# Seven products instead of eight in more pairs of a feed-forward layer, with sums made by accumulating transfers

## The chip, the cores and the metric

The kernel runs on one core of a Trainium2 chip. A core has TensorE (PE in the profile; its weight loads are PEld), VectorE (DVE), ScalarE (ACT), GpSimd (POOL) and SyncE (SP), each with its own queue of instructions, worked off in order. TensorE writes only to PSUM, which has eight banks of 512 float32 columns. SP and ACT issue plain transfers (DMAs); transfers that add to their destination are issued by GpSimd here. The metric is the device time of one execution in microseconds; less is better.

## The reference

The reference is a decoder trunk of two layers over 256 tokens and 2048 features in float32: a dilated sliding-window attention layer, then a latent attention layer, each followed by a residual SwiGLU feed-forward part, and a last RMS norm:

```python
h = x
for layer in range(DEPTH):
    xn = rms_norm(h, attn_norm_g[layer])
    h = h + (dilated_attention(xn, ...) if layer < 1 else mla_attention(xn, ...))
    h = h + swiglu(rms_norm(h, ffn_norm_g[layer]), ffn_w_gu[layer], ffn_w_down[layer])
return rms_norm(h, final_norm_g)

def swiglu(xn, w_gu, w_down):
    g, u = jnp.split(xn @ w_gu, 2, axis=-1)     # each 2048 -> 5632
    return (jax.nn.silu(g) * u) @ w_down         # 5632 -> 2048
```

## The kernel before

**Weights.** All weights stream from HBM once, in units of up to 1 MB (128 partitions x 2048 float32). SP loads a unit into one of three `raw` buffers. Each float32 value is then split into two float32r parts: ScalarE casts `raw` to `hi`, VectorE subtracts to get `lo`. `hi` and `lo` have three buffers each, because splitting runs two units ahead of TensorE (`ahead=2`), and loads run as far as raw buffers come free (`WeightStream`, L82 to L211). A product of x and w is three matmuls of 512 columns: xh by wh, xh by wl, xl by wh (`mul`, L687 to L691).

**Feed-forward.** The hidden width is worked in three parts of 16, 16 and 12 chunks of 128 (`FFN_PARTS`). Within a part, groups of four chunks (512 columns of gate and the same 512 of up) are made by `mixed`, with 8 units each: unit kp holds two k-chunks of gate and up, so its raw tile has four blocks of 512 columns. A group's result is gated (`swiglu`, L743), put in SBUF as `up`, transposed by TensorE and split into `hT` (`turned`, L750). Then down products for pairs of 512 output columns follow, by `mixed` again with 8 units; the third part uses plain products. There are 11 groups and 4 such down products in each of the two layers.

**Seven products.** Two token halves, two k-chunks and two weight columns make a 2x2 by 2x2 block product: eight products of blocks, or seven with Winograd's sums. A unit marked "seven" uses sums of x (`sums`, L656, made once and kept in `forms` and `forms_h`) and of w. In `split_blocks` (L172) such a unit casts and splits three blocks as `hi` and `lo`, makes four in-place sums of 512 columns on VectorE (L185 to L188), and casts and splits the four sums as `th` and `tl`, which have one buffer. Four of the seven products go to four PSUM banks `pb`, three to the accumulators `la` and `ra`. After a group's last seven-unit the banks are combined: `gate` and `up` get the partial sums (L716 to L721), and the accumulators are added to them afterwards (L739), or, in down, the partial sums are added to the residual `h` by an accumulating transfer from the GpSimd queue (L766). Before, units kp = 2, 4, 6 are "seven" in every gate-and-up group but a layer's first, and kp = 2, 5 in down products of 16 chunks.

**PSUM.** `ps_acc` has two accumulators of two banks, `ps_one` four single banks. The transposes in `turned` take two banks of `ps_one`.

**Order.** The program is written in one order; a scheduler that knows priorities by that order, waits and free buffers fixes each engine's queue before the run. Work that is to come later is put off by units: `later.put(n, ...)` runs it after n more units (`later.tick()`). `turned` comes one unit after its group.

Of the kernel before, what the change touches and what calls it, by code (L numbers as in the profile page):

```python
# [10 lines left out]
F32 = mybir.dt.float32  # L11
# [6 lines left out]
P = 128  # L18
S = 256
# [28 lines left out]
SEVEN = (2, 4, 6)  # L48
SEVEN_DOWN = {16: (2, 5), 12: ()}
# [38 lines left out]
class WeightStream:  # L88
# [10 lines left out]
    def load(self, upto):  # L99
        while self.n_raw < min(upto, len(self.units)):  # L100
            ap, _, form = self.units[self.n_raw]
            t = self.raw_pool.tile([P, 2048], F32, tag="raw", name="raw", bufs=self.raw_bufs)
            if form in ("eight", "seven"):
                v = t.rearrange("p (k n c) -> p k n c", n=2, c=512)
                for n in range(2):
                    self.nc.sync.dma_start(out=v[:, :, 1 - n, :], in_=ap[n])
                self.raws[self.n_raw] = t
                self.n_raw += 1
                continue
# [60 lines left out]
    def split_blocks(self, raw, form):  # L170
# [4 lines left out]
        blk = lambda t, i: t[:, i * 512:(i + 1) * 512]  # L175
# [8 lines left out]
        tt = self.nc.vector.tensor_tensor  # L184
        tt(out=b22, in0=b22, in1=b12, op=ALU.subtract)  # L185
# [37 lines left out]
def kernel(ctx, tc, consts, x, attn_norm_g, ffn_norm_g, a_w_qkv, a_w_o, kv_norm_g,  # L223
# [55 lines left out]
    def load_rest():  # L279

        nc.sync.dma_start(out=cst_a[0], in_=consts[:, C_M0:])
        nc.sync.dma_start(out=cst, in_=consts[:, C_MB:C_M0])
# [82 lines left out]
    cst, cst_a = cpool.tile([P, C_M0 - C_MB], F32, name="cst"), []  # L365
    later.put(3, load_rest)

    def con(at, n, rows=P):
        t, base = (cst, C_MB) if at < C_M0 else (cst_a[0], C_M0)
        return t[:rows, at - base:at - base + n]  # L370

    cos_b, sin_b = con(C_CB, S), con(C_SB, S)
# [57 lines left out]
    def across(r, name):  # L430

        dg = tmp.tile([P, S], F32, tag="diag", name="diag", bufs=1)
        for t in range(NT):
            nc.vector.tensor_scalar(out=dg[:, t * P:(t + 1) * P], in0=ident, scalar1=r[:, t:t + 1],
                                    scalar2=None, op0=ALU.mult)
        ps = bank()
        mm(out=ps[:, :S], lhsT=ones, rhs=dg, start=True, stop=True)
        R = small.tile([P, S], F32, name=name, tag=name, bufs=1)
# [202 lines left out]
    def ffn(xT, rstd, finish):  # L641

        with tc.tile_pool(name="ffn", bufs=1) as fp:
# [11 lines left out]
            forms_h = fp.tile([P, 2, 2, 3, P], F32R, name="forms_h")  # L655
# [319 lines left out]
```

## Time and profile before

| what | us |
|---|---|
| median of 3 runs (lowest, highest) | 2673.95 (2673.07, 2676.16) |
| span of the profiled execution | 2672.9 |
| median less that span (outside it) | 1.05 |
| TensorE busy | 2655.3 |
| VectorE busy | 2020.8 |
| ScalarE busy | 1295.8 |
| GpSimd busy | 24.9 |

The span is from the first to the last instruction. The first feed-forward part takes the time from about 1000 to 1690 us, the second from about 1980 to the end. Matmuls overlap, so a busy TensorE is not one at its peak; the distance between the starts of two matmuls is what one costs. In a row of a group, the numbers after the bar are busy time, mean ns of one, and the idle time of the engine just before, with what ended it. The granted TensorE clock was 0.998 of full speed.

### The profile page before, as it was taken

The page shows a single profiled execution, that of the slowest core. Times are in us where ns is not written, and L with a number is a line of the kernel's source. Part 1 is how long each engine was busy: PE and PEld are TensorE (multiplying, and loading weights), DVE is VectorE, ACT ScalarE, POOL GpSimd, SP SyncE. Part 2 cuts the span into 40 slices and gives each one's busy share as a digit, 9 for nine tenths or more (in the row PEclk, how much of TensorE's full clock was granted, in tenths as well). Part 3 has the DMA queues.
Part 4 walks back from the last instruction along what each step waited for, and adds up shares of the span by engine and source line. Part 5 has one row for each costly group of instructions (what it writes and reads, how often), then busy time and mean ns, then how long its engine had stood idle before and what let it go on. Part 6 is the DMA issues. An engine that isn't in the chain of part 4 may idle for free.

```text
span 2672.9 us, 32983 instructions
## 1 busy us (share of the span) xinstructions
PE 2655.3 (99%) x12938; PEld 2228.0 (83%) x12938; DVE 2020.8 (76%) x2758; ACT 1295.8 (48%) x1649; POOL 24.9 (1%) x28
## 2 busy tenths in 40 slices
PE   9999999999999999999999999999999999999998
PEld 7888888888888888888888888888888888888887
DVE  5676577477477668988998896588579978997985
ACT  5444444434444445544554454565445544554553
POOL 0000000000000000000000000000000000000000
PEclk9999999999999999999999999999999999999999
DMA  7545545554555555566566756444555576657663
GB/s 271 190 158 171 192 159 173 189 174 164 174 183 165 198 188 190 184 210 221 185 211 211 227 175 203 157 143 140 177 180 189 189 230 199 217 188 222 204 215 133
DMA packets 308091, 504.20 MB, mean 189 GB/s; under 512 B 13960, under 2 KB 117088, under 8 KB 307552
## 3 DMA queue, kind: packets, MB, share of 16 engines
q1 hardware_dynamic: 302960, 492.64, 55.2%
q0 software_dynamic: 4352, 8.39, 1.7%
q8 instruction: 101, 1.65, 0.3%
q10 hardware_dynamic: 624, 1.07, 0.1%
q14 instruction: 54, 0.44, 0.0%
HBM read 491.57 MB, written 2.10 MB: 185 GB/s over the span
## 4 chain that ended last, share of the span: by engine, by line
PE 87%; DVE 6%; DMA 3%; issue 2%; ACT 2%; SPq 0%; POOL 0%; ACTq 0%; DVEq 0%; POOLq 0%
PE acc L451 14%; PE acc L689 10%; PE acc L690 10%; PE acc L691 10%; PE acc L471 8%; PE acc L470 8%; PE acc L472 8%; PE acc L454 7%; DVE lo L168 2%; PE bank L689 2%; PE bank L691 2%; PE bank L690 2%; DMA raw<-in_ffn_w_gu_dram 1%; DMA raw<-in_ffn_w_down_dram 1%; PE bank L566 1%
## 5 line engine op out<-in xcount | busy, mean ns | idle before, releaser
L158 DVE TENSOR_TENSOR lo<-raw,hi 128x1024 fp32r<-128x1024 f32 (+2 forms) x450 | 515.7, 1166 | 347.3 <-ACT hi L157 331.3
L157 ACT CAST hi<-raw 128x1024 fp32r<-128x1024 f32 (+2 forms) x450 | 432.6, 1006 | 550.0 <-PE acc L451 297.4
L167 ACT CAST hi<-raw 128x1024 fp32r<-128x1024 f32 (+1 forms) x404 | 443.8, 1130 | 384.3 <-PE acc L691 146.4
L168 DVE TENSOR_TENSOR lo<-raw,hi 128x1024 fp32r<-128x1024 f32 (+1 forms) x404 | 526.2, 1321 | 110.0 <-ACT hi L167 108.8
L689 PE MATMUL acc<-hi,xT_f 128*128 128x512 f32 x988 | 387.2, 392 | 0.4 <-DVE gate L739 0.4
L691 PE MATMUL acc<-hi,xT_f 128*128 128x512 f32 x988 | 385.4, 390 | 0.0
L690 PE MATMUL acc<-lo,xT_f 128*128 128x512 f32 x988 | 385.0, 390 | 0.0
L451 PE MATMUL acc<-xT_a,hi 128*128 128x512 f32 x1536 | 379.4, 395 | 0.0
L451 PEld LDWEIGHTS acc<-xT_a,hi 128*128 128x128 f32 x1536 | 281.6, 188 | 53.8
L689 PEld LDWEIGHTS acc<-hi,xT_f 128*128 128x128 f32 x988 | 185.5, 188 | 41.8 <-issue 2.5
L167 ACT CAST th<-raw 128x1024 fp32r<-128x1024 f32 x152 | 154.0, 1049 | 133.4 <-DVE raw L187 122.3
L691 PEld LDWEIGHTS acc<-hi,xT_f 128*128 128x128 f32 x988 | 185.5, 188 | 39.1
L690 PEld LDWEIGHTS acc<-lo,xT_f 128*128 128x128 f32 x988 | 185.6, 188 | 38.2
L454 PEld LDWEIGHTS acc<-xT_a,lo 128*128 128x128 f32 x1536 | 196.9, 191 | 7.6
L454 PE MATMUL acc<-xT_a,lo 128*128 128x256 f32 x1536 | 199.2, 283 | 0.0
L168 DVE TENSOR_TENSOR tl<-raw,th 128x1024 fp32r<-128x1024 f32 x152 | 180.5, 1221 | 12.6 <-ACT th L167 12.4
L689 PE MATMUL acc<-hi,hT 128*128 128x512 f32 x400 | 156.4, 391 | 1.5 <-DVE gate L739 1.0
L691 PE MATMUL acc<-hi,hT 128*128 128x512 f32 x400 | 155.9, 390 | 0.0
L690 PE MATMUL acc<-lo,hT 128*128 128x512 f32 x400 | 155.8, 390 | 0.0
L471 PE MATMUL acc<-lo,xT_a 128*128 128x512 f32 x384 | 150.6, 392 | 0.8 <-DVE lo L158 0.8
L472 PE MATMUL acc<-hi,xT_a 128*128 128x512 f32 x384 | 150.9, 393 | 0.0
L470 PE MATMUL acc<-hi,xT_a 128*128 128x512 f32 x384 | 150.8, 393 | 0.0
(274 smaller groups left out, 3942.6 us busy)
## 6 DMA issues: line engine op xcount, KB each, us to landing
raw<-in_ffn_w_gu_dram SPq DMA_DIRECT2D x352, 512.0 KB, 4.5
raw<-in_a_w_qkv_dram SPq DMA_DIRECT2D x143, 1024.0 KB, 4.9
raw<-in_ffn_w_down_dram SPq DMA_DIRECT2D x128, 512.0 KB, 5.0
raw<-in_ffn_w_down_dram SPq DMA_DIRECT2D x24, 1024.0 KB, 5.1
raw<-in_a_w_o_dram SPq DMA_DIRECT2D x16, 1024.0 KB, 5.0
raw<-in_b_w_o_dram SPq DMA_DIRECT2D x16, 1024.0 KB, 5.1
raw<-in_b_w_kv_b_dram SPq DMA_DIRECT2D x8, 1024.0 KB, 5.3
raw<-in_b_w_q_b_dram SPq DMA_DIRECT2D x8, 768.0 KB, 4.5
```

What stands on the lines that cost most here:

```text
L157: nc.scalar.copy(out=h, in_=src)
L158: nc.vector.tensor_tensor(out=l, in0=src, in1=h.bitcast(F32), op=ALU.subtract)
L167: self.nc.scalar.copy(out=hi, in_=src)
L168: self.nc.vector.tensor_tensor(out=lo, in0=src, in1=hi.bitcast(F32), op=ALU.subtract)
L451: mm(out=acc[:, i, :], lhsT=sl(hi, kk), rhs=xT[:, k0 + kk, :], start=first and kk == 0, stop=False)
L454: mm(out=acc[:, i, 0:S], lhsT=sl(lo, kk), rhs=xT[:, k0 + kk, 0:S], start=False, stop=last and kk == nk - 1)
L470: mm(out=acc[:, t, :ncol], lhsT=xh, rhs=rhs(hi, kk), start=st, stop=False)
L471: mm(out=acc[:, t, :ncol], lhsT=xh, rhs=rhs(lo, kk), start=False, stop=False)
L472: mm(out=acc[:, t, :ncol], lhsT=xl, rhs=rhs(hi, kk), start=False, stop=sp)
L689: mm(out=out, lhsT=xh, rhs=wh, start=st, stop=False)
L690: mm(out=out, lhsT=xh, rhs=wl, start=False, stop=False)
L691: mm(out=out, lhsT=xl, rhs=wh, start=False, stop=sp)
```

## The change

- **Which pairs.** In gate and up kp = 0, 2, 4, 6 are seven-product pairs (20 groups), in the down products of 16 chunks kp = 2, 4, 6 (8 of them).
- **The sums of w.** The two plain loads of a unit change places. For a "seven" unit GpSimd issues a third transfer that reads one block of 128 x 512 from HBM again and adds it to the block beside it in `raw`. After that all four blocks are cast and split whole, one in-place difference of 512 columns and one of 2 x 512 follow, and three blocks are cast and split as `th` and `tl`. One sum of x has its sign turned.
- **Whole tiles.** An eight-product unit is cast in one instruction of 2048 columns and subtracted in one, where it was two of 1024.
- **Products.** The seven products come in another order: to `pb[0]`, `la`, `pb[1]`, `ra`, `pb[3]`, `pb[2]`, `la`. Since a group may now begin with a seven-unit, the accumulators' start flags are kept by name (`first`). The four banks are taken at kp = 0 of a gate-and-up group.
- **Combining.** One copy on ScalarE, two sums of 512 columns and one of 2 x 512; `gate` has a third block for it and `u2` is gone.
- **The up half.** In a group that is neither a layer's first nor a part's last, the up accumulator is copied to SBUF by ScalarE (`whole`), and GpSimd issues a transfer that adds `up` to it; the product with gate follows two units later and `turned` three.
- **Memory.** `across` uses its result tile for the diagonal, and the constants of the second attention are loaded when that begins, not with the first ones.

```diff
-SEVEN = (2, 4, 6)
-SEVEN_DOWN = {16: (2, 5), 12: ()}
+SEVEN = (0, 2, 4, 6)
+SEVEN_DOWN = {16: (2, 4, 6), 12: ()}
...
-                for n in range(2):
+                for n in (1, 0):
                     self.nc.sync.dma_start(out=v[:, :, 1 - n, :], in_=ap[n])
+                if form == "seven":
+                    self.nc.gpsimd.dma_start(out=v[:, 0, 0, :], in_=ap[0][:, 0, :], accum_op=ALU.add)
...
-            for i in (slice(0, 1024), slice(1024, 2048)):
-                self.halve(hi[:, i], lo[:, i], raw[:, i])
+        self.halve(hi, lo, raw)
...
-        i = slice(512, 2048)
-        self.halve(hi[:, i], lo[:, i], raw[:, i])
-        th, tl = [self.sum_pool.tile([P, 2048], F32R, tag=n, name=n, bufs=1) for n in ("th", "tl")]
-        b12, b11, b22, b21 = [blk(raw, j) for j in range(4)]
-        tt(out=b22, in0=b22, in1=b12, op=ALU.subtract)
-        tt(out=b12, in0=b12, in1=b11, op=ALU.subtract)
-        tt(out=b11, in0=b11, in1=b22, op=ALU.add)
-        tt(out=b21, in0=b21, in1=b11, op=ALU.subtract)
-        for i in (slice(0, 1024), slice(1024, 2048)):
-            self.halve(th[:, i], tl[:, i], raw[:, i])
+        th, tl = [self.sum_pool.tile([P, 1536], F32R, tag=n, name=n, bufs=1) for n in ("th", "tl")]
+        v = raw.rearrange("p (i c) -> p i c", c=512)
+        self.nc.vector.tensor_tensor(out=v[:, 2], in0=v[:, 0], in1=v[:, 2], op=ALU.subtract)
+        self.nc.vector.tensor_tensor(out=v[:, 1::2], in0=v[:, 1::2],
+                                     in1=v[:, 2].unsqueeze(1).broadcast_to([P, 2, 512]), op=ALU.subtract)
+        self.halve(th, tl, raw[:, 512:])
...
                         mul(pb[0], x(0, 0), w[:2], 1, st, sp)
-                        mul(la[:, 0], x(0, 1), w[:2], 3, False, False)
-                        mul(ra[:, 0], y(3), w[:2], 2, False, False)
-                        mul(la[:, 1], x(1, 1), w[2:], 3, False, False)
-                        mul(pb[1], y(0), w[2:], 0, st, sp)
+                        mul(la[:, 0], x(0, 1), w[:2], 3, first("la0"), False)
+                        mul(pb[1], y(0), w[:2], 0, st, sp)
+                        mul(ra[:, 0], y(3), w[:2], 2, first("ra0"), False)
+                        mul(pb[3], y(2), w[2:], 0, st, sp)
                         mul(pb[2], y(1), w[2:], 1, st, sp)
-                        mul(pb[3], y(2), w[2:], 2, st, sp)
+                        mul(la[:, 1], x(1, 1), w[2:], 2, first("la1"), False)
...
-                        u2 = fp.tile([P, 512], F32, tag="u2", name="u2")
                         nc.scalar.copy(out=left[:, 0], in_=pb[0])
-                        for o, x_, y_ in ((u2, pb[2], left[:, 0]), (left[:, 1], pb[3], u2),
-                                          (right[:, 0], pb[1], u2), (right[:, 1], pb[1], left[:, 1])):
-                            nc.vector.tensor_tensor(out=o, in0=x_, in1=y_, op=ALU.add)
+                        nc.vector.tensor_tensor(out=left[:, 1], in0=pb[2], in1=left[:, 0], op=ALU.add)
+                        nc.vector.tensor_tensor(out=left[:, 2], in0=pb[3], in1=left[:, 1], op=ALU.add)
+                        nc.vector.tensor_tensor(out=right, in0=pb[1].unsqueeze(1).broadcast_to([P, NT, 512]),
+                                                in1=left[:, 1:3], op=ALU.subtract)
...
+                    if not first:
+                        nc.vector.tensor_tensor(out=gate, in0=g, in1=gate, op=ALU.add)
+                        g = gate
+                    if first or ended:
+                        if not first:
+                            nc.vector.tensor_tensor(out=up, in0=u, in1=up, op=ALU.add)
+                            u = up
+                        silu(g)
+                        gated(u)
+                        later.put(1, turned)
+                    else:
+                        whole = fp.tile([P, NT, 512], F32, tag="whole", name="whole")
+                        nc.scalar.copy(out=whole, in_=u)
+                        nc.gpsimd.dma_start(out=whole, in_=up, accum_op=ALU.add)
+                        silu(g)
+                        later.put(2, lambda gated=gated, whole=whole: gated(whole))
+                        later.put(3, turned)
...
+        cst_b.append(bp.tile([P, C_M0 - C_MB], F32, name="cst_b", bufs=1))
+        nc.sync.dma_start(out=cst_b[0], in_=consts[:, C_MB:C_M0])
```

More of the change, by code (lines that the diff above doesn't have):

```diff
@@ L281, in load_rest @@
         nc.sync.dma_start(out=cst_a[0], in_=consts[:, C_M0:])
-        nc.sync.dma_start(out=cst, in_=consts[:, C_MB:C_M0])
         row = cpool.tile([sum(n_rest), P], F32, name="g_row")
@@ L363 @@
         ws.load(i + 1)
-    cst, cst_a = cpool.tile([P, C_M0 - C_MB], F32, name="cst"), []
+    cst_a, cst_b = [], []
     later.put(3, load_rest)
     def con(at, n, rows=P):
-        t, base = (cst, C_MB) if at < C_M0 else (cst_a[0], C_M0)
+        t, base = (cst_b[0], C_MB) if at < C_M0 else (cst_a[0], C_M0)
         return t[:rows, at - base:at - base + n]
-    cos_b, sin_b = con(C_CB, S), con(C_SB, S)
     mhalf = cpool.tile([P, NT], F32, name="mhalf")
@@ L430, in across @@
     def across(r, name):
-        dg = tmp.tile([P, S], F32, tag="diag", name="diag", bufs=1)
+        R = small.tile([P, S], F32, name=name, tag=name, bufs=1)
         for t in range(NT):
-            nc.vector.tensor_scalar(out=dg[:, t * P:(t + 1) * P], in0=ident, scalar1=r[:, t:t + 1],
+            nc.vector.tensor_scalar(out=R[:, t * P:(t + 1) * P], in0=ident, scalar1=r[:, t:t + 1],
                                     scalar2=None, op0=ALU.mult)
         ps = bank()
-        mm(out=ps[:, :S], lhsT=ones, rhs=dg, start=True, stop=True)
-        R = small.tile([P, S], F32, name=name, tag=name, bufs=1)
+        mm(out=ps[:, :S], lhsT=ones, rhs=R, start=True, stop=True)
         nc.vector.tensor_copy(out=R, in_=ps[:, :S])
@@ L653, in ffn @@
             forms = fp.tile([P, len(SEVEN), 2, 3, P], F32R, name="forms")
-            forms_h = fp.tile([P, 2, 2, 3, P], F32R, name="forms_h")
+            forms_h = fp.tile([P, 3, 2, 3, P], F32R, name="forms_h")
             def sums(x, kp, d):
@@ L684, in mixed, with first @@
                 la, ra = acc_tile(), acc_tile()
-                pb = None
+                pb, begun = None, set()
+                def first(m):
+                    new = m not in begun
+                    begun.add(m)
+                    return new
                 def mul(out, x, w, i, st, sp):
@@ L736, in ffn, with silu, gated @@
                     g, u = mixed(xT, KD // 2, () if first else SEVEN, forms, gate, up)
-                    if not first:
-                        for acc, d in ((g, gate), (u, up)):
-                            nc.vector.tensor_tensor(out=d, in0=acc, in1=d, op=ALU.add)
-                        g, u = gate, up
+                    gate = gate[:, 0:3:2]
+                    ended = j + 4 == n
                     sc_ = rstd if first else rem
-                    def swiglu(g=g, u=u, gate=gate, up=up, sc_=sc_):
+                    def silu(g, gate=gate, sc_=sc_):
                         for t in range(NT):
                             nc.scalar.activation(out=gate[:, t], in_=g[:, t], func=AF.Silu, scale=sc_[:, t:t + 1])
+                    def gated(u, gate=gate, up=up, sc_=sc_):
                         for t in range(NT):
@@ L764, in ffn @@
                                                     op=ALU.add)
-                    for i, part_sum in enumerate((left, right)):
+                    for i, part_sum in enumerate((left[:, 0:3:2], right)):
                         nc.gpsimd.dma_start(out=h[:, :, (c + i) * 512:(c + i + 1) * 512], in_=part_sum,
```

15 lines of the change are left out of this document (6 added, 9 removed).

## The prediction

> **What bounds the kernel now.** I read the page's busy times and chain first, then the feed-forward stage by windows, then one gate-and-up column group in the timeline, then the groups by shape, and last the waits of the DMA queues.
>
> ```profile
> PE 2655.3 (99%) x12938; PEld 2228.0 (83%) x12938; DVE 2020.8 (76%) x2758; ACT 1295.8 (48%) x1649; POOL 24.9 (1%) x28
> PE 87%; DVE 6%; DMA 3%; issue 2%; ACT 2%; SPq 0%; POOL 0%; ACTq 0%; DVEq 0%; POOLq 0%
> 1300.00:1400.00 100.00, 99.48 (x443) 81.36 (x442) 94.00 (x109) 55.76 (x60) 0.00 (x0) 1.00 0.60 200
> 1537.60:1579.90 42.30, 42.30 (x191) 34.84 (x191) 39.00 (x41) 22.40 (x25) 0.00 (x0) 1.00 0.60 199
> ```
>
> The first line is busy time, the second the chain that ended last. The last two are windows: length, then busy PE, weight load, VectorE, ScalarE, GpSimd, granted clock, DMA share. TensorE sets the end. But inside the feed-forward part VectorE works 94 of 100 us; in one column group (42.3 us) 39.0, with 3.3 to spare. So a matmul removed there is worth its time only if VectorE needs no more.
>
> The timeline gives what a matmul costs. Its durations overlap, so starts are counted.
>
> ```profile
> 1505.20 0.39 PE L689 MATMUL bank<-hi,xT_f 128*128 128x512 f32 x1
> 1510.03 0.39 PE L689 MATMUL acc<-hi,xT_f 128*128 128x512 f32 x1
> 1515.48 0.39 PE L689 MATMUL bank<-hi,xT_f 128*128 128x512 f32 x1
> L718 ACT COPY gate<-bank 128x512 f32<-128x512 f32 x28 | 16.1, 575 | 0.0
> 1541.66 0.87 PE bank L405 x8
> 1584.32 0.87 PE bank L405 x8
> ```
>
> A seven-product pair (21 matmuls) runs from 1505.20 to 1510.03, 4.83 us; the eight-product pair after it (24) to 1515.48, 5.45 us. The last two rows, of the chain in order of time, are the transposes of two successive column groups: 42.66 us apart, which is 5 x 5.45 + 3 x 4.83 + 0.87 = 42.6. TensorE loses nothing there.
>
> **The change, part by part.** *Products.* One evacuation row per product group that has seven-product pairs: x28, that is 20 gate-and-up groups and 8 down groups. Each gets one more such pair: 28 x (5.45 - 4.83) = 17.4 us off TensorE. That is the whole possible gain through TensorE. The order inside a pair and the start flags move no matmul in or out.
>
> *VectorE and ScalarE.*
>
> ```profile
> L158 DVE TENSOR_TENSOR lo<-raw,hi 128x1024 fp32r<-128x1024 f32 x414 | 496.2, 1218 | 347.3 <-ACT hi L157 331.3 <-PE acc L454 15.7
> L168 DVE TENSOR_TENSOR lo<-raw,hi 128x1024 fp32r<-128x1024 f32 x328 | 393.0, 1220 | 68.6 <-ACT hi L167 67.6
> L168 DVE TENSOR_TENSOR lo<-raw,hi 128x1536 fp32r<-128x1536 f32 x76 | 133.5, 1756 | 41.4 <-ACT hi L167 41.2
> L185 DVE TENSOR_TENSOR raw<-raw 128x512 f32<-128x512 f32 x76 | 52.5, 690 | 2.1
> L167 ACT CAST hi<-raw 128x1024 fp32r<-128x1024 f32 x328 | 331.4, 1050 | 284.4 <-PE acc L691 112.0 <-DMA raw<-in_ffn_w_gu_dram 76.0 <-issue 65.3
> L167 ACT CAST hi<-raw 128x1536 fp32r<-128x1536 f32 x76 | 112.4, 1479 | 99.9 <-issue 35.3 <-PE acc L691 34.4 <-DMA raw<-in_ffn_w_down_dram 20.8
> L721 DVE TENSOR_TENSOR u<-bank,gate 128x512 f32<-128x512 f32 x28 | 19.2, 684 | 1.4 <-PE bank L691 1.4
> L739 DVE TENSOR_TENSOR up<-acc,up 128x1024 f32<-128x1024 f32 x20 | 24.5, 1223 | 6.9 <-PE acc L691 6.7
> L747 DVE SCALAR_TENSOR_TENSOR up<-up,rem,gate 128x512 f32<-128x512 f32 x40 | 28.3, 749 | 1.9
> L381 DVE TENSOR_TENSOR hT<-bank,hT 128x512 fp32r<-128x512 f32 x44 | 29.6, 684 | 0.0
> L667 DVE TENSOR_TENSOR g<-f 128x128 f32<-128x128 f32 x28 | 6.8, 285 | 0.2
> ```
>
> From 1024 to 1536 columns the subtraction grows by 0.54 us and the cast by 0.43, so whole 2048-column tiles are estimated at 2.29 and 1.91 us. VectorE per column group before: five eight-pairs of 2 x 1.22, three seven-pairs of 1.76 + 4 x 0.69 + 2 x 1.22 = 6.96, evacuation 4 x 0.68, two joins of 1.22, two products of 0.75, two halves of hT of 0.68: 12.2 + 20.9 + 2.7 + 2.4 + 1.5 + 1.4 = 41.1 us (39.0 in the window: neighbours overlap by some 0.05 us). After: eight-pair 2.29; seven-pair 2.29 + 0.69 + 1.22 + 1.76 = 5.96; evacuation 0.68 + 0.68 + 1.22; one join: 9.2 + 23.8 + 2.6 + 1.2 + 1.5 + 1.4 = 39.7, with 28 instructions instead of 41. So VectorE needs 1.4 us less where TensorE needs 0.6 less: it stays just under. In a down group it goes from 34.0 to 34.7 us of 41.7: covered. Three more preparations of token sums per layer add about 0.7 + 4 x 0.29 and two subtractions each, some 3 us, in groups with free time on VectorE: nothing, or at most 6 x 3 = 18 us were none of it covered; I take nothing. ScalarE per group goes from 22.4 by one copy of 1024 columns (1.05) and a seven-pair more to about 24 of 42: covered.
>
> *Accumulating transfers.* A seven-pair's raw tile is complete only when the GpSimd queue's transfer, which waits for the first plain load, has landed. Nothing in this trace accumulates from HBM; the nearest rows are the 512 KB sums into h.
>
> ```profile
> L106 SPq DMA_DIRECT2D raw<-in_ffn_w_gu_dram x16: 367/420/472, 1503.5 to 1532.8; - x16
> DMA to landing us min/median/max: 3.7/4.6/6.3
> L766 POOL DMA_DIRECT2D h<-gate x8: 1200/1200/1356, 1194.5 to 2469.8; - x8
> DMA to landing us min/median/max: 5.8/6.7/8.0
> q1 hardware_dynamic: 302960, 492.64, 55.2%
> q0 software_dynamic: 4352, 8.39, 1.7%
> SPq L106 <- DVE tl L168: 526.6, 72, 14.2
> ACT hi L167 <- DMA raw<-in_ffn_w_gu_dram: 76.0, 40, 4.1
> ```
>
> The two landing lines belong to the tile raw from 1500 to 1545 us and to the line of the h sums. 1.7% of 2672.9 us over 16 transfers is 2.8 us of moving each; half the bytes save 1.4, so an accumulate takes 4.4 to 6.6 us from issue. Hence a seven-pair's tile is ready 3.7 + 4.4 = 8.1 to 4.6 + 6.6 = 11.2 us after its buffer came free, an eight-pair's after about 5. There are three raw buffers. A seven-pair holds one for 8.1 to 11.2 plus 1.91 + 2.29 + 0.69 + 1.22 + 1.48 + 1.76 = 9.35, an eight-pair for 5 + 4.2: together 26.7 to 29.8 us of the 3 x 10.28 = 30.8 that two pairs offer. Before it was 5 + 1.48 + 1.76 + 2.76 + 1.05 + 1.22 = 13.3 or more against 8.5, 21.8 us. Loads waited for the buffers already (the third line from below, and ScalarE for loads 76 us in all, without stopping TensorE). Direct cost if it fits: nothing, covered by the two pairs that are split ahead; if not, the second rival. The DMA engines get 104 x 256 KB and 14 x 512 KB more, 34.6 MB at q0's rate: 7% of the span on top of 57%. Covered.
>
> The Trainium skill ("DMA: Bandwidth & Descriptors", Anatomy of one DMA) gives 2.0 us plus the bytes at 436 GB/s for such a DMA. By it 512 KB take 3.2 us, where the trace has 5.8 to 8.0; 256 KB would take 2.6 and the holding would be 24.9 us or less. The rows decide, and their margin is the thin one.
>
> *The up half.* Instead of a join (1.22 on VectorE), a ScalarE copy and a 512 KB accumulate of 5.8 to 8.0 us; the product with gate comes two pairs, 10.3 us, later. It fits, by 1 to 3 us if GpSimd isn't itself waiting for a raw tile at that moment.
>
> *Banks.* The four banks are now held from the first pair to the seventh, so the transposes of the group before, due within them, can run only when the copy of the first product and the first sum have emptied two, late in pair six or in pair seven. TensorE is in order: each of 20 groups may wait there, or for the first accumulators, between nothing and one whole cast that stands in the way on ScalarE (1.91 us).
>
> ```profile
>   PE acc L689: 1.4, 5
> L489 ACT COPY t<-acc 128x512 f32<-128x512 f32 x64 | 37.5, 587 | 10.4 <-PE acc L454 10.4
> ```
>
> The first row: in five of 20 groups TensorE waited 0.3 us for the join at L739. I take 0.4 us in each group, nearer the low end because three other products can go first: 20 x 0.4 = 8 us.
>
> *The moved constants* (448 KB, SP queue) load while the second attention begins, two latent products before rotation and masks need them: nothing; at most one load's landing, 6.3 us.
>
> Sum: 2672.9 - 17.4 + 8 = 2663.5 of span; the median of the runs is 1.05 us above the profiled span, so **2664.5**.
>
> **The rivals.** *First: the boundary eats it.* If TensorE waits 0.8 us in each group (a ScalarE cast half done), 16 us go and 2672.5 stands: no change. For it: the transposes now depend on two evacuations on two engines, behind casts that depend on transfers. Against: the waiting product can be overtaken by products into other banks.
>
> *Second, on the other side: the raw buffers throttle.* It is decided when two pairs hold buffers longer than 30.8 us. At the upper end (29.8) 1 us of queueing suffices, and an eight-pair's subtraction can stand behind a seven-pair's two differences (1.9 us). Held 32 us, each two pairs lose 1.2 / 3 = 0.4 us; four times in 20 groups 32 us: 2673.95 - 17.4 + 32 = 2688. For it: loads already land when ScalarE wants them, and a late tile blocks ScalarE's queue, behind which stand evacuation and copy. Against: the low end leaves 4 us. That GpSimd's issues are slowed by a busy VectorE speaks little: they took 1.20 us, at most 1.36, in the row above.
>
> *Third: the change doesn't do what it says*, VectorE's relief being lost because the gating product stands ahead of splits in its queue and waits for the joining transfer. In 14 groups with a join by transfer, 1.22 us of saved work then comes back as a wait, 17 us: 2674, no change.
>
> **How the numbers follow.** Forecast 0.52 (own range 2656 to 2668); boundary 0.13, third 0.08; throttle 0.27. What a measurement can tell from no change is 0.2%, 5.3 us: faster below 2668.6, slower above 2679.3. Faster 0.52, same 0.21, slower 0.27. Lower end of the range: all 17.4 us and a few us of today's small stops, 2654; upper end: the throttle's own 2688 and a little more, 2690; longer throttles are the tail left out.
>
> **What would show it.** Right: a steady group near 42.0 us, the seven-pairs' cast waiting for a GpSimd transfer without a gap on TensorE, VectorE at 38 to 39 us a group. Boundary: gaps at L405 and at the first accumulators. Throttle: gaps where th or hi is first used, SP waiting for buffers longer than before, VectorE below 85%. The forecast is wrong if an accumulate takes over 7 us, or if VectorE's 2048-column subtraction is far from 2.29 us.

## The result and the profile after

The changed kernel takes 2834.38 us (median of 4 runs, 2827.44 to 2845.12) where the kernel before took 2673.61 beside it: 1.0606 times the time [1.0583, 1.0629], 160.8 us more. One of the four runs of the kernel with four raw buffers and whole tiles took 3931.29 us at a granted clock of 0.63; its ratio is that of the other three (2727.66 to 2732.61). The prediction was 2664.5 us, with a range up to 2690. It was wrong in sign and size.

From the page of the changed kernel: busy times, the chain that ended last, and the traffic of the GpSimd queue.

```profile
span 2825.7 us, 32763 instructions
PE 2705.1 (96%) x12854; PEld 2231.9 (79%) x12854; DVE 2027.7 (72%) x2450; ACT 1333.2 (47%) x1463; POOL 127.7 (5%) x146
q0 software_dynamic: 21344, 43.00, 9.5%
PE 57%; DMA 22%; DVE 11%; ACT 5%; issue 4%; SPq 0%; POOLq 0%; ACTq 0%; DVEq 0%; POOL 0%
```

The change did what it says: 84 matmuls fewer (28 products of three), 34.6 MB more on the GpSimd queue. But 22% of the chain is now transfers, where it was 3%. Against the page before, TensorE's idle time (span less busy) grew from 17.6 to 120.6 us and its busy time by 49.8 us, although it has less to do; the two are the 152.8 us by which the span grew. Why TensorE is busy longer with fewer matmuls comes in the last section.

Windows of the same steady stretch that the prediction read (length, busy PE, weight load, VectorE, ScalarE, GpSimd, clock, DMA share):

```profile
1300.00:1400.00 100.00, 91.66 (x378) 71.80 (x378) 76.33 (x55) 50.24 (x37) 8.60 (x10) 0.95 0.71 201
```

378 matmuls started in these 100 us, where it was 443. VectorE, which had 94.00 us of work there, has 76.33. So no engine is at its limit, and yet everything is late: it looks like a latency that goes round, not like a busy engine. The costs of single instructions were as estimated:

```profile
L169 ACT CAST hi<-raw 128x2048 fp32r<-128x2048 f32 x240 | 457.8, 1910 | 506.7 <-DMA raw<-in_ffn_w_gu_dram 252.9
L170 DVE TENSOR_TENSOR lo<-raw,hi 128x2048 fp32r<-128x2048 f32 x240 | 548.8, 2288 | 185.3 <-ACT hi L169 184.5
```

The waits of the engines, of the SP queue and of TensorE (total, times, longest) tell who is late:

```profile
ACT hi L169 <- DMA raw<-in_ffn_w_gu_dram: 252.9, 95, 7.1
ACT hi L169 <- DMA raw<-in_ffn_w_down_dram: 110.8, 34, 7.3
DVE up L744 <- DMA whole<-up: 65.1, 14, 6.4
SPq L106 <- DVE lo L170: 769.1, 126, 12.1
SPq L106 <- DVE tl L170: 150.9, 99, 4.7
PE bank L686 <- ACT th L169: 23.4, 17, 2.1
PE bank L687 <- DVE tl L170: 19.5, 22, 1.6
PE acc L687 <- DVE lo L170: 19.0, 10, 2.6
PE bank L398 <- ACT gate L714: 14.9, 9, 2.9
PE acc L686 <- DVE gate L753: 9.1, 4, 2.6
```

ScalarE waited 252.9 us for gate-and-up tiles, where it was 76.0, and TensorE waits where th, tl and lo are first used. Not only seven-pairs are late: lo is, too. The last two rows are TensorE's waits at the transposes (for the copy that empties a bank) and at a product's first accumulators (for VectorE's join), 24 us together. SP's waits for VectorE to free a buffer didn't grow. In the kernel before, lo has a row of its own beside the 526.6 us for tl:

```profile
SPq L106 <- DVE lo L168: 433.7, 154, 6.4
```

That is 960.3 us before and 920.0 after. What grew is SP's waits before loads that ended with a transfer's landing, from 58.5 to 219.8 us.

The accumulating transfers themselves, by their two lines: issues on GpSimd, and the time from issue to landing, for the weights (first two) and for the joining transfer of up.

```profile
L108 POOL DMA_DIRECT2D raw<-in_ffn_w_gu_dram x80: 859/859/1038, 1004.1 to 2720.3; - x80
DMA to landing us min/median/max: 4.0/4.3/7.7
L765 POOL DMA_DIRECT2D whole<-up x14: 861/863/877, 1070.9 to 2698.1; - x14
DMA to landing us min/median/max: 7.3/8.5/9.3
```

The estimates were 4.4 to 6.6 us for the first, where the median is 4.3, and 5.8 to 8.0 for the second, which is too low.

**One raw buffer, followed round.** The timeline of the changed kernel, 1322 to 1345 us, on SP, GpSimd, ScalarE and VectorE (start, duration, engine, line; in brackets the idle time before):

```profile
1322.23 1.75 DVE L170 TENSOR_TENSOR tl<-raw,th 128x1536 fp32r<-128x1536 f32 x1
1324.00 0.88 SPq L106 DMA_DIRECT2D raw<-in_ffn_w_gu_dram  x2
1330.58 0.86 POOL L108 DMA_DIRECT2D raw<-in_ffn_w_gu_dram  x1 [10.86 <-DMA raw<-in_ffn_w_gu_dram]
1334.90 1.91 ACT L169 CAST hi<-raw 128x2048 fp32r<-128x2048 f32 x1 [4.01 <-DMA raw<-in_ffn_w_gu_dram]
1336.84 2.29 DVE L170 TENSOR_TENSOR lo<-raw,hi 128x2048 fp32r<-128x2048 f32 x1 [3.49 <-ACT hi L169]
1339.90 1.23 DVE L183 TENSOR_TENSOR raw<-raw 128x1024 f32<-128x1024 f32 x1
1341.04 2.28 DVE L170 TENSOR_TENSOR lo<-raw,hi 128x2048 fp32r<-128x2048 f32 x1
1343.24 1.75 DVE L170 TENSOR_TENSOR tl<-raw,th 128x1536 fp32r<-128x1536 f32 x1
...
1329.39 2.29 DVE L170 TENSOR_TENSOR lo<-raw,hi 128x2048 fp32r<-128x2048 f32 x1
1331.71 0.98 SPq L106 DMA_DIRECT2D raw<-in_ffn_w_gu_dram  x2
1338.04 1.92 ACT L169 CAST hi<-raw 128x2048 fp32r<-128x2048 f32 x1 [1.23 <-DMA raw<-in_ffn_w_gu_dram]
```

A buffer comes free at 1323.98, when a tl has been made. SP loads at once; GpSimd issues the accumulate 6.6 us later, when the plain load that it waits for has landed, it lands 4.3 us after that, and the cast starts at 1334.90, 10.9 us after the buffer was free. Then cast, subtraction, two differences and th follow one another, with an eight-pair's lo put in between, and the buffer is free again at 1344.99: held 21.0 us. The eight-pair's buffer, free at 1331.68, has its tile at 1338.04 and is free at 1343.32: held 11.6 us. Together 32.6, more than the 30.8 that three buffers offer in two pairs. Each buffer is loaded again the moment it is free, so this sum is the length of the round itself; that the number of buffers sets it, and not an engine behind them, is tried below with a fourth. This is one of the milder cycles: four tl follow one another from 1308.5 to 1343.2, so that two pairs take 11.6 us on average instead of 10.28.

### The profile page after: what moved, and what is told of

Read it like the earlier page. It is cut to its first block, busy times and chain, and to the rows that moved or that the text cites. A ratio compares the mean times of both kernels' runs of the same rounds, so it can differ in the third digit from the quotient of the medians.

```text
span 2825.7 us, 32763 instructions
## 1 busy us (share of the span) xinstructions
PE 2705.1 (96%) x12854; PEld 2231.9 (79%) x12854; DVE 2027.7 (72%) x2450; ACT 1333.2 (47%) x1463; POOL 127.7 (5%) x146
## 4 chain that ended last, share of the span: by engine, by line
PE 57%; DMA 22%; DVE 11%; ACT 5%; issue 4%; SPq 0%; POOLq 0%; ACTq 0%; DVEq 0%; POOL 0%
DMA raw<-in_ffn_w_gu_dram 15%; PE acc L443 14%; PE acc L462 7%; PE acc L463 7%; PE acc L464 7%; PE acc L446 7%; DMA raw<-in_ffn_w_down_dram 5%; DVE lo L170 5%; ACT hi L169 4%; PE acc L686 3%; PE acc L687 3%; PE acc L688 3%; DVE tl L170 2%; DMA whole<-up 2%; PE bank L558 1%
## 5 line engine op out<-in xcount | busy, mean ns | idle before, releaser
L169 ACT CAST hi<-raw 128x2048 fp32r<-128x2048 f32 x240 | 457.8, 1910 | 506.7 <-DMA raw<-in_ffn_w_gu_dram 252.9
L170 DVE TENSOR_TENSOR lo<-raw,hi 128x2048 fp32r<-128x2048 f32 x240 | 548.8, 2288 | 185.3 <-ACT hi L169 184.5
L687 PE MATMUL acc<-lo,xT_f 128*128 128x512 f32 x848 | 338.4, 399 | 19.0 <-DVE lo L170 19.0
L686 PE MATMUL acc<-hi,xT_f 128*128 128x512 f32 x848 | 340.7, 402 | 0.4 <-ACT whole L764 0.2
L688 PE MATMUL acc<-hi,xT_f 128*128 128x512 f32 x848 | 335.4, 397 | 0.0
L169 ACT CAST th<-raw 128x1536 fp32r<-128x1536 f32 x104 | 153.5, 1476 | 150.6 <-DVE raw L183 145.6
L170 DVE TENSOR_TENSOR tl<-raw,th 128x1536 fp32r<-128x1536 f32 x104 | 182.3, 1753 | 38.8 <-ACT th L169 38.8
L687 PEld LDWEIGHTS acc<-lo,xT_f 128*128 128x128 f32 x848 | 163.4, 193 | 57.9 <-DVE lo L170 23.4
L686 PEld LDWEIGHTS acc<-hi,xT_f 128*128 128x128 f32 x848 | 163.5, 193 | 41.7 <-ACT whole L764 6.1
L688 PEld LDWEIGHTS acc<-hi,xT_f 128*128 128x128 f32 x848 | 162.9, 192 | 35.2
L686 PE MATMUL acc<-hi,hT 128*128 128x512 f32 x344 | 136.9, 398 | 12.9 <-DVE gate L753 9.1
L687 PE MATMUL acc<-lo,hT 128*128 128x512 f32 x344 | 135.2, 393 | 0.0
L688 PE MATMUL acc<-hi,hT 128*128 128x512 f32 x344 | 135.0, 392 | 0.0
```

What stands on the lines that cost most here:

```text
L169: self.nc.scalar.copy(out=hi, in_=src)
L170: self.nc.vector.tensor_tensor(out=lo, in0=src, in1=hi.bitcast(F32), op=ALU.subtract)
L686: mm(out=out, lhsT=xh, rhs=wh, start=st, stop=False)
L687: mm(out=out, lhsT=xh, rhs=wl, start=False, stop=False)
L688: mm(out=out, lhsT=xl, rhs=wh, start=False, stop=sp)
```

## The experiments

In the expectations, A is the theory that late weight tiles hold the three raw buffers too long (the second rival). Against it stand the joining transfer of up, the load and the long instructions of VectorE and ScalarE, and the four seven-pairs themselves. Each ratio is to the kernel before, run beside it.

### Which accumulating transfer: four kernels

*The sum of the weights on VectorE*, just ahead of the split, so that a tile is complete with its plain loads:

```diff
-                if form == "seven":
-                    self.nc.gpsimd.dma_start(out=v[:, 0, 0, :], in_=ap[0][:, 0, :], accum_op=ALU.add)
...
+        if form == "seven":
+            self.nc.vector.tensor_tensor(out=raw[:, :512], in0=raw[:, :512], in1=raw[:, 512:1024], op=ALU.add)
         self.halve(hi, lo, raw)
```

> The changed kernel, but the weight sum of a seven-product pair is an addition of 512 columns on VectorE (0.69 us each, 104 of them) and not an accumulating transfer. Theory A (the transfer makes the raw tile late, and three raw buffers can't cover it): the tile is ready about 5 us after its buffer comes free and not 8 to 11, most of the 160 us goes away, 2680 to 2720 us. Theory B (the four banks held from the first pair and the up half joined by a transfer hold TensorE up): both are still there, over 2790 us.

Measured: 2772.19 us, 1.0365 [1.035, 1.0381]. 62 us come back, though VectorE has 104 instructions more. But A's 2680 to 2720 was missed: the transfers are not all of it.

*The up half joined on VectorE again*, with the transfers of the weights left as they are:

```diff
-                    if first or ended:
+                    if True:
```

> The changed kernel, but every group's up half is joined by VectorE as before the change, without the copy and the joining transfer, and its transposes are due one pair later, not three. Theory A: the weight transfers stay and set the pace, 2790 to 2840 us. Theory B: the join's part of the loss goes, 14 waits of some 5 us each, and with the banks still held 2740 to 2780 us.

Measured: 2819.55 us, 1.0549 [1.0531, 1.0566]: 15 us back. The joining transfer costs something, but little of the whole.

*Both edits together:*

```diff
-                    self.nc.gpsimd.dma_start(out=v[:, 0, 0, :], in_=ap[0][:, 0, :], accum_op=ALU.add)
...
+            self.nc.vector.tensor_tensor(out=raw[:, :512], in0=raw[:, :512], in1=raw[:, 512:1024], op=ALU.add)
...
-                    if first or ended:
+                    if True:
```

> The changed kernel with both sums on VectorE, so that no accumulating transfer is left beside those into h; the pairs, the order of products and the banks are the changed ones. Theory A: 2665 to 2710 us, and VectorE, with 43.7 us of work in a group for TensorE's 42.0, sets the pace rather than the raw buffers: about 1.7 us a group over, 20 groups, 2690 us. Theory B (banks alone): over 2750 us.

Measured: 2759.05 us, 1.0321 [1.0303, 1.034]. With both transfers gone, 86 us are still lost, and A's 2665 to 2710 was missed, so there is a second cause.

*The sum of the weights left out*, without anything in its place. This prices the weight transfers without loading VectorE:

```diff
-                if form == "seven":
-                    self.nc.gpsimd.dma_start(out=v[:, 0, 0, :], in_=ap[0][:, 0, :], accum_op=ALU.add)
```

> The changed kernel with the weight sum left out altogether: the accumulating transfers of the weights are gone and nothing stands in their place, so the output lacks that sum; every other instruction is there. Theory A: the raw tile is ready 5 us after its buffer is free and VectorE has its 39.7 us a group, so the predicted gain comes out, 2655 to 2690 us. Theory B: the rest of the change holds TensorE up without the transfers too, over 2780 us.

Measured: 2751.06 us, 1.0294 [1.0278, 1.0309]. The weight transfers cost 83 us of the 161; 78 are left without them, between the ranges of A and B. A window of this kernel, and the products that wait for th there (grouped by shape, 1000 to 1690 us):

```profile
1250.00:1350.00 100.00, 95.56 (x408) 75.59 (x406) 77.29 (x56) 52.26 (x36) 3.01 (x4) 0.98 0.66 199
L684 PE MATMUL bank<-th,forms 128*128 128x512 f32 x80 | 30.9, 429 | 10.7 <-ACT th L167 10.7
```

VectorE works 77.29 of 100 us and TensorE still waits for what it and ScalarE make. So the rest isn't load either; the reading that fits is the time that a tile takes through cast, subtraction, differences, th and tl.

### What the other 78 us are: four kernels

The first three start from the kernel without the sum of the weights. *Half tiles:* hi and lo in two instructions of 1024 columns, th and tl in two of 768.

```diff
-        self.halve(hi, lo, raw)
+        for i in (slice(0, 1024), slice(1024, 2048)):
+            self.halve(hi[:, i], lo[:, i], raw[:, i])
...
-        self.halve(th, tl, raw[:, 512:])
+        for i in (slice(0, 768), slice(768, 1536)):
+            self.halve(th[:, i], tl[:, i], raw[:, 512:][:, i])
```

> The kernel without the weight sum (its output lacks that sum), and the whole-tile casts and subtractions cut in two again: hi and lo by 1024 columns, th and tl by 768. Theory C (an instruction of 1.9 or 2.3 us that can't be interrupted is put ahead of the short chain of differences, th and tl, and TensorE waits for th, tl and lo): most of the 77 us left there go, 2665 to 2700 us. Theory D (the fourth pair is at fault: banks, transposes, seven-pairs two units apart throughout): within 15 us of the kernel without the sum, about 2750 us.

Measured: 2746.09 us, 1.0274 [1.0259, 1.0289], 5 us back. Alone, the length of the instructions is not it.

*The pairs of before:*

```diff
-SEVEN = (0, 2, 4, 6)
-SEVEN_DOWN = {16: (2, 4, 6), 12: ()}
+SEVEN = (2, 4, 6)
+SEVEN_DOWN = {16: (2, 5), 12: ()}
```

> The kernel without the weight sum (its output lacks that sum), with the pairs of before (2, 4, 6 in gate and up, 2 and 5 in down), so that the four banks are taken at the third unit and three eight-product pairs stand together at a group's edge; TensorE has 17 us more to do. Theory C: the long instructions are still there, and only the longer edge helps, 2710 to 2750 us. Theory D: 2670 to 2695 us, TensorE's old time.

Measured: 2705.84 us, 1.0123 [1.0108, 1.0139]: 45 us faster with 17.4 us more of TensorE work, outside both ranges. The 28 added seven-pairs cost more than they save; those in gate and up are taken out by themselves further down.

*The up half joined on VectorE*, the sum of the weights still left out:

```diff
-                    if first or ended:
+                    if True:
```

> The kernel without the weight sum (its output lacks that sum), with the up half joined on VectorE: no copy, no joining transfer, transposes due one pair later. Theory C and theory D: the join is a small part, as between the changed kernel and that with the join on VectorE (15 us): 2735 to 2755 us. If the joining transfer is what holds the rest: below 2700 us.

Measured: 2722.5 us, 1.0188 [1.0171, 1.0205]: 29 us back, more than either theory allowed, and twice what the same edit brought with late weight tiles (these may have covered a part of it). In a timeline of the changed kernel VectorE stands for it:

```profile
1316.95 0.75 DVE L744 SCALAR_TENSOR_TENSOR up<-whole,rem,gate 128x512 f32<-128x512 f32 x1 [3.34 <-DMA whole<-up]
```

*Half tiles where both sums are VectorE's*, the halves of the first edit put into the kernel with both sums on VectorE:

```diff
-        self.halve(hi, lo, raw)
+        for i in (slice(0, 1024), slice(1024, 2048)):
+            self.halve(hi[:, i], lo[:, i], raw[:, i])
...
-        self.halve(th, tl, raw[:, 512:])
+        for i in (slice(0, 768), slice(768, 1536)):
+            self.halve(th[:, i], tl[:, i], raw[:, 512:][:, i])
```

> Both sums on VectorE, the four pairs kept, and the casts and subtractions cut in two again. Nothing is left out. Theory C: 2670 to 2710 us, although VectorE has some 0.2 us more to do in each unit. Theory D: about 2760 us, as with both sums on VectorE and whole tiles.

Measured: 2708.18 us, 1.013 [1.0114, 1.0146], 51 us back where the same cut brought 5. In a window the kernel with whole tiles had VectorE at 88.63 of 100 us:

```profile
1300.00:1400.00 100.00, 93.19 (x393) 73.83 (x393) 88.63 (x77) 51.20 (x38) 0.00 (x0) 0.95 0.53 175
```

A long instruction that stands ahead hurts where the queue is full. That this is why the two differ is the reading that fits, not shown by itself.

### Buffers: three or four

A fourth buffer of 8 KB per partition needs room. This kernel makes it: up joined on VectorE, (2, 5) in down, the first partial sum in a small shared tile, so that `gate` has two blocks again. The weights' transfers and the four pairs stay.

```diff
-SEVEN_DOWN = {16: (2, 4, 6), 12: ()}
+SEVEN_DOWN = {16: (2, 5), 12: ()}
...
+                        u2 = tmp.tile([P, 2, S], F32, tag="t1", name="u2").rearrange("p a b -> p (a b)")
+                        nc.vector.tensor_tensor(out=u2, in0=pb[2], in1=left[:, 0], op=ALU.add)
...
-                return [fp.tile([P, n, 512], F32, tag=m, name=m) for m, n in (("gate", NT + 1), ("up", NT))]
+                return [fp.tile([P, n, 512], F32, tag=m, name=m) for m, n in (("gate", NT), ("up", NT))]
...
-                    if first or ended:
+                    if True:
```

> The weight transfers and the four pairs kept; the up half joined on VectorE, down pairs 2 and 5, and the first sum of an evacuation in a small shared tile, all of which only makes room in SBUF. Control of the next kernel, three raw buffers. Theory A and any other: about as the changed kernel with the join on VectorE, 2800 to 2830 us.

Measured: 2863.48 us, 1.0722 [1.0706, 1.0738], with the three buffers. It is slower than the changed kernel although the joining transfer is gone, and 44 us slower than that kernel with the join on VectorE (2819.55). Why is open in part: TensorE waited 35.2 us in all for the join before a product's first accumulators, where it was 14.3 there.

*The same with a fourth buffer and nothing else:*

```diff
-    ws = WeightStream(nc, rawp, hlp, units, raw_bufs=3, ahead=2)
+    ws = WeightStream(nc, rawp, hlp, units, raw_bufs=4, ahead=2)
```

> The same with four raw buffers instead of three, and nothing else. Theory A (a raw tile that is late because its buffer comes free late and the transfer adds 3 to 6 us, three buffers being too few): the load starts a unit earlier, so nearly all that the transfers cost, some 80 to 100 us, goes: 2710 to 2745 us, near the kernel without the sum and with the join on VectorE (2722 us). Theory E (the transfers cost by standing in line, on GpSimd or before ScalarE's cast, whatever the buffers): over 2780 us.

Measured: 2731.64 us, 1.0219 [1.0202, 1.0236]. One buffer more takes 132 us away, with every transfer and instruction as it was. That is A's case: what costs is the holding of buffers, since the DMA engines and GpSimd have the same to do in both. With the transfers it is now 9 us above the kernel with three buffers, without the weight sum and with the same join (2722.5), and of these, 5 us are the eight seven-pairs in down that it lacks. Whether a fourth buffer would also help a kernel without late tiles wasn't tried, and the control is slow for another reason too, so 132 us isn't the price of the transfers alone.

*Three buffers, the transfers, and the pairs of before:*

```diff
-SEVEN = (0, 2, 4, 6)
-SEVEN_DOWN = {16: (2, 4, 6), 12: ()}
+SEVEN = (2, 4, 6)
+SEVEN_DOWN = {16: (2, 5), 12: ()}
```

> The changed kernel with the pairs of before (2, 4, 6 and 2, 5), transfers and whole tiles and the joining transfer kept; 17 us more for TensorE. Theory A: the transfers still cost, though less since three eight-product pairs stand together at a group's edge: 2740 to 2780 us, that is 35 to 75 us over the same without the weight sum (2706 us). Theory D (the fourth pair does nearly all): 2705 to 2720 us.

Measured: 2804.27 us, 1.0493 [1.0475, 1.051]. Against the kernel with these pairs and without the transfers (2705.84), 98 us, more than the 35 to 75 expected: the throttle doesn't need the fourth pair.

*Only the down pairs of the change*: both sums on VectorE, half tiles, three pairs in gate and up.

```diff
-SEVEN = (0, 2, 4, 6)
+SEVEN = (2, 4, 6)
```

> A version that might be faster than both: both sums on VectorE, casts and subtractions cut in two, pairs 2, 4, 6 in gate and up as before, and 2, 4, 6 in down, where VectorE has free time; eight pairs more than before with 0.62 us each, 5 us. If theories A, C and D together are the whole story: 2665 to 2678 us. If the new order of products or the new evacuation costs by itself: over 2685 us.

Measured: 2696.04 us, 1.0089 [1.0074, 1.0104]. It missed 2665 to 2678. 12 us less than with the fourth pair, yet still slower than before.

### What is left, and what beats both

*Order of products and new evacuation alone:* the pairs of before, no sum of weights, up on VectorE, half tiles. Against the last one:

```diff
-SEVEN_DOWN = {16: (2, 4, 6), 12: ()}
+SEVEN_DOWN = {16: (2, 5), 12: ()}
...
-        if form == "seven":
-            self.nc.vector.tensor_tensor(out=raw[:, :512], in0=raw[:, :512], in1=raw[:, 512:1024], op=ALU.add)
```

> The weight sum left out (its output lacks that sum), the pairs of before, the up half joined on VectorE, casts and subtractions cut in two: what stays of the change is the new order of products, the new evacuation, and two differences in place of four sums. If transfers, fourth pair, joining transfer and long instructions are all of the loss (theories A, C, D): 2660 to 2680 us, TensorE's old time. If order or evacuation cost by themselves: 2690 to 2705 us, as the version with sevens in down only (2696 us).

Measured: 2679.34 us, 1.0027 [1.0017, 1.0037]. The order of the products, the other evacuation and the smaller rest of the change cost about 7 us together. The banks are held as before here, from pair two.

*Four buffers and half tiles*, the weights' transfers and the four pairs kept:

```diff
-        self.halve(hi, lo, raw)
+        for i in (slice(0, 1024), slice(1024, 2048)):
+            self.halve(hi[:, i], lo[:, i], raw[:, i])
...
-        self.halve(th, tl, raw[:, 512:])
+        for i in (slice(0, 768), slice(768, 1536)):
+            self.halve(th[:, i], tl[:, i], raw[:, 512:][:, i])
```

> The kernel with four raw buffers (weight transfers, four pairs, join on VectorE; 2732 us) with the casts and subtractions cut in two. Theory C (long instructions ahead of the th and tl chain): 2670 to 2705 us. Theory D (the fourth pair itself): 2720 to 2735 us.

Measured: 2694.78 us, 1.0081 [1.0065, 1.0098], 37 us back from half tiles, as theory C had it. TensorE's largest wait in it (total, times, longest), and a window:

```profile
PE acc L688 <- DVE gate L756: 15.7, 4, 3.9
1300.00:1400.00 100.00, 98.04 (x429) 77.96 (x428) 91.63 (x102) 55.55 (x66) 6.88 (x8) 1.00 0.73 220
```

*The same with three pairs in gate and up, and (2, 4, 6) in down:*

```diff
-SEVEN = (0, 2, 4, 6)
-SEVEN_DOWN = {16: (2, 5), 12: ()}
+SEVEN = (2, 4, 6)
+SEVEN_DOWN = {16: (2, 4, 6), 12: ()}
```

> The same with pairs 2, 4, 6 in gate and up and 2, 4, 6 in down; VectorE has some 2.5 us a group less than before the change, and TensorE 5 us less in all. Theory A with C and D: the transfers are covered by the fourth buffer, 2662 to 2680 us. If the new order or evacuation cost by themselves: 2690 us or more.

Measured: 2665.11 us (7 runs, 2664.5 to 2665.76), 0.9972 [0.9961, 0.9983]: faster than before, by 7.7 us, and the only one that beats both kernels. Its page, its window, the landing of its weight transfers, and who waited for plain loads:

```profile
PE 2649.1 (99%) x12914; PEld 2222.9 (83%) x12914; DVE 1993.1 (75%) x2742; ACT 1318.4 (50%) x1749; POOL 98.0 (4%) x112
PE 98%; DVE 1%; issue 1%; ACT 1%; DMA 0%; SPq 0%; POOL 0%; POOLq 0%; DVEq 0%; ACTq 0%
1300.00:1400.00 100.00, 100.00 (x446) 81.99 (x445) 89.37 (x103) 55.87 (x68) 6.01 (x7) 1.00 0.70 217
L108 POOL DMA_DIRECT2D raw<-in_ffn_w_gu_dram x60: 859/862/1036, 1007.6 to 2561.3; - x60
DMA to landing us min/median/max: 4.3/5.8/7.1
  POOL raw L108: 750.4, 55
```

The transfers land later here than in the changed kernel (5.8 us against 4.3), and TensorE is busy 100.00 of 100 us: with a buffer more they are covered. The last row is all that waits for the plain loads, the GpSimd queue; ScalarE no longer does. VectorE has less to do than in the kernel before, 1993.1 us against 2020.8.

*Where the fourth pair costs.* A group that closes a part is followed by down products, which wait for it. Here these groups (6 of 20) have three seven-pairs and the others four. In those six the sums of pair 0's tokens, already in place, are used by an ordinary eight-pair, which alters the output and leaves no instruction out.

```diff
-                    units.append((blocks, None, "seven" if j > 0 and kp in SEVEN else "eight"))
+                    units.append((blocks, None, "seven" if j > 0 and kp in SEVEN[j + 4 == k0 + n:] else "eight"))
...
-                    g, u = mixed(xT, KD // 2, () if first else SEVEN, forms, gate, up)
+                    skip = int(j + 4 == n)
+                    g, u = mixed(xT, KD // 2, () if first else SEVEN[skip:], forms[:, skip:], gate, up)
```

> Four raw buffers, tiles cut in two, four pairs, except in the last group of each part (6 groups), which has pairs 2, 4, 6: there the transposes of the group before find free banks before the four are taken. TensorE has 6 x 0.62 = 3.7 us more to do than with four pairs everywhere (2694.8 us). If the edge to the down products holds the loss: 2668 to 2684 us. If every group with a fourth pair loses some 1.5 us: 2688 to 2696 us.

Measured: 2687.61 us, 1.0064 [1.0047, 1.0081]; 7 us less by the medians, 4.5 by the ratios, and between the two ranges. Three pairs in all groups, with one more in each down product, had brought 30. But this doesn't clear the turn to the down products: the wait has moved. With four pairs in all groups, TensorE's four waits of 3.9 us stand at the first down product of the four parts whose down products have seven-pairs. Here four of 3.6 us stand one group earlier, where the part's last group now begins with an eight-pair. From the timelines of the first such place, with four pairs in all groups (first three rows) and here (last row):

```profile
1141.89 0.66 PE L400 MATMUL bank<-ident,up 128*128 128x128 f32 x4
1147.16 0.69 DVE L656 TENSOR_TENSOR f<-hT 128x512 f32<-128x512 f32 x1
1153.13 1.21 DVE L756 TENSOR_TENSOR gate<-acc,gate 128x1024 f32<-128x1024 f32 x1
1109.78 0.77 PE L688 MATMUL acc<-hi,xT_f 128*128 128x512 f32 x1 [3.62 <-DVE gate L757]
```

The last group of that part begins at 1105.98. Its four banks are taken from pair 0 on, so the transposes of the group before run 36 us into it, at 1141.89; with three pairs in all groups they ran 5.5 us into it. What VectorE makes of them, up to the token sums for down (L656 and on), then stands just ahead of the evacuation and of the join at L756. An eight-pair writes to an accumulator with its first matmul, and so waits for that join, which began 3.0 us after the start of the group's last matmul; with three pairs it began 1.1 us before it. The third part of a layer, whose down products have no token sums, shows no such wait.

Elsewhere the fourth pair does no such harm: with four pairs the transposes of successive groups are 42.4 to 43.0 us apart, with three 42.8. Only into the last group of those four parts it is 44.5 to 45.2. So the cost isn't in every group; it lies at the ends of four parts, and by the order of the rows it comes from the banks that are taken at pair 0. With four buffers and half tiles no matmul waited for th or tl, and weight loads only 3.1 us for th, so their single buffer isn't it. No run moves the transposes or the token sums alone, and whether a VectorE with less than 91.63 us of work in 100 would hide them is open.

## Why the prediction was wrong

**The step that failed** is that on the accumulating transfers: the holding of 26.7 to 29.8 us against 30.8, and its conclusion "Direct cost if it fits: nothing". The way was right: hold per buffer against buffers times period. The terms were durations without the waits between them. The seven-pair's tile was ready 10.9 us after its buffer came free (8.1 to 11.2 had been estimated), but its work took 10.1 instead of 9.35; the eight-pair's tile was ready after 6.4 instead of 5 and its work took 5.3 instead of 4.2. That is 32.6 (21.0 and 11.6). With 1 us of room at the upper end, as the prediction itself had seen, queueing alone decides. Three of its figures were also misread or mis-summed: the 526.6 us of SP's waits are those for tl alone (960.3 with lo), ScalarE's 76 us those for gate-and-up loads alone (107.0 with down), and the holding with 2.6 us for an accumulate comes to 24.9 to 25.8, not to 24.9 or less.

**The second rival** named the mechanism, and two of its signs came: gaps at th and tl, and VectorE at 76%. The third, SP waiting longer for buffers, came only in part: all its waits before these loads rose from 1067.8 to 1207.3 us, but those for VectorE's lo and tl fell. But its price, 0.4 us for two pairs, came out of an assumed holding of 32 us. Measured were 1.3 us in the stretch shown, and over the kernel 83 and 98 us in two comparisons with and without the transfers, 132 in that of the buffers. Its 32 us over the kernel were 2.6 to 4 times too small, and it stood at 0.27 where the rows left a margin of 1 to 4 us in 30.8.

**The second step that failed** is VectorE's: "it stays just under", 39.7 us in 42.0. As a load this was nearly right: VectorE has 2027.7 us of work for 2020.8 before (the prediction's terms add up to about 4 us less), and it is never the bound. But a relief in load isn't one in latency. Where there were two instructions of 1.22 us, one of 2.29 lets the next engine wait for a whole tile; half tiles brought 5, 51 and 37 us in three kernels. With four buffers and half tiles the fourth pair still costs: going to three gained 29.7 us although TensorE got 12.4 - 5.0 = 7.4 more to do (20 pairs given up in gate and up, 8 taken in down, 0.62 us each), so it is 37 us.

**The third rival** was real and small: the gating product does stand ahead of splits and waits for the joining transfer, 65.1 us in 14 groups, 4.7 each. 17 us were priced; 15 came back in the changed kernel, 29 without the weight transfers. The transfer took 8.5 us where the estimate ended at 8.0, but that is only half a microsecond. The larger error is the time that was thought to be there: in the stretch shown the copy of the up accumulator ended at 1308.40 and VectorE stood ready for the product at 1313.61, 5.2 us later and not 10.3.

**The boundary** is the third step that was mis-sized, at 0.4 us a group or 8 us in the sum. The first rival's signs came: in the changed kernel 24 us of TensorE's waits are at the transposes and at first accumulators, where the rival had 16. With four buffers and half tiles, where little else is in the way, it is the bulk of the fourth pair's 37 us: four waits of 3.9 us, each followed by up to 3.4 us at half clock, and some 2 us more into the last group of each of the four parts, about 31 us in all. The prediction priced it evenly over 20 groups; it falls where the next product begins with an eight-pair.

**What was right:** 17.4 us from TensorE's side (the best version shows its share: 24 matmuls fewer, 8 x 0.62 = 5.0 us, where 7.7 were measured), the cast and the subtraction of 2048 columns, the landing of the weight transfers (4.3 us, at the low edge). Of the two signs that were to show the forecast wrong, another subtraction stayed away; an accumulate over 7 us came, as one of the 104 weight transfers (7.7 us at most) and as the joining transfer (8.5), but not where the loss is. Both signs tested the terms, not the waits between them.

## What to carry to other kernels

When a tile's way into the kernel gets one more step, add up how long each buffer is held, from free to free, with the waits inside, and compare it with buffers times period; if the margin is as thin as here (1 to 4 us in 30.8), take it as missing, and buy the buffer first. An engine's load in a steady window says whether it can keep up, not whether its results come in time: a queue of long instructions at 77% of its time can still stop TensorE. Taking banks earlier also puts off whoever else needs them, and the work that hangs on that arrives where the next product waits. And a change in several parts is to be tried in parts: here the transfers with three pairs in the down products gained together, once there was a fourth buffer, and the fourth pair in gate and up and the whole tiles lost.

## What the runs showed of the hardware

A stall of TensorE costs more than itself. A timeline of the changed kernel on TensorE, and a window over what follows:

```profile
1368.42 0.40 PE L686 MATMUL acc<-hi,xT_f 128*128 128x512 f32 x1
1370.75 0.50 PE L687 MATMUL acc<-lo,xT_f 128*128 128x512 f32 x1 [1.93 <-DVE lo L170]
1371.09 0.40 PE L688 MATMUL acc<-hi,xT_f 128*128 128x512 f32 x1
1373.44 1.22 PE L686 MATMUL bank<-th,forms 128*128 128x512 f32 x2 [1.96 <-ACT th L169]
1374.88 0.63 PE L686 MATMUL acc<-hi,xT_f 128*128 128x512 f32 x1
1375.31 0.63 PE L687 MATMUL acc<-lo,xT_f 128*128 128x512 f32 x1
1372.20:1379.00 6.80, 5.56 (x13) 4.40 (x14) 5.80 (x5) 3.08 (x2) 0.00 (x0) 0.50 0.60 202
```

Two waits of 1.9 us, and from 1372.2 on the granted clock is 0.50: matmuls start 0.43 us apart instead of 0.23, for 6.8 us. In the kernel with four buffers and half tiles, a wait of 3.92 us was followed by 3.4 us of it:

```profile
1154.49 0.47 PE L688 MATMUL acc<-hi,hT 128*128 128x512 f32 x1 [3.92 <-DVE gate L756]
1155.60:1159.00 3.40, 3.40 (x10) 2.63 (x9) 3.37 (x5) 0.11 (x1) 0.00 (x0) 0.50 0.14 26
```

Over the changed kernel the mean granted clock is 0.982, before 0.998: 0.018 x 2825.7 less 0.002 x 2672.9 is 45 us of full clock that weren't granted, part of them while TensorE stood still anyway. So it is at most 45 of the 67 us (49.8 and the 17.4 of work taken out) by which TensorE is busier than its work; the rest no row here explains. The prediction had counted a stall at its own length. The Trainium skill ("TensorE: Matmul & The Clock Gate", Part 1: The HAM clock gate) says that the clock falls to half after an idle window of some 3.4 us, windows that run freely. The length of the slow stretches and the half agree with these rows; that a whole window must be idle doesn't: between 1368.4 and 1372.2 two matmuls ran.

The two accumulating transfers differ about as their bytes do: 256 KB from HBM land 4.3 us after issue, 512 KB from SBUF to SBUF 8.5 us, at the same 0.86 us of GpSimd. But the bytes aren't all: the 512 KB sums into h landed after 6.7 us in the kernel before.
